# Stick-breaking attention: weights taken as differences of one scan, summed by parts

## The chip, the cores and the metric

The kernel runs on one core of a Trainium2 chip. The metric is the device time of one launch in microseconds (us), as the median of several runs; the kernel before takes 988.35 us (three runs, 987.6 to 989.67).

## The reference

One layer of a streaming encoder. The prompt has 1024 tokens, and 64 new tokens of a running stream have a past of 512; both are computed in the same launch. Per token: RMS norm, one input projection from 1024 to 6144 columns (queries, keys, values and a SiLU gate z for each of two attention branches of 8 heads of 64, and two merge gates), the two attentions, their projections, a gated sum and an output projection with the residual. The branch that is changed is stick breaking:

```python
z = einsum("bqhd,bkhd->bhqk", q, k) * 0.125          # causal: key position < query position
log_keep = where(causal, log_sigmoid(-z), 0.0)
suffix = cumsum(log_keep, axis=3, reverse=True) - log_keep
w = where(causal, exp(log_sigmoid(z) + suffix), 0.0)
out = einsum("bhqk,bkhd->bqhd", w, v)
```

In words: with keep = sigmoid(-z) the weight of key s is sigmoid(z[s]) times the product of keep over all keys between s and the query. Call P[s] the product of keep from s up to the query. Then the weight of s is also P[s+1] - P[s].

## The kernel before

All large products are split into a high and a low part of the fast float format, three matmuls for one. The work has five phases: a first projection by rows (line 464), a second projection computed with seven block products in place of eight (line 634), the two attentions with the remaining eight projection units woven in (lines 663 to 1231), the branch projections, and the output projection.

**The second projection** (lines 544 to 657) takes 12 column pairs with seven steps each, 84 steps of 24 matmuls. `prep` cuts a block of weights into halves five steps ahead of its use: ScalarE makes the high half, GpSimd the low one. `emit` evaluates finished sums into one of four `hl` buffers, and `soon` and `step` put the stores of these into SyncE's queue at the next step. SyncE issues nearly all transfers of the kernel in program order; an issue that has to wait holds back all behind it.

**The attention loop** (line 1189) goes over 136 items: first stick breaking, then band attention, in each four pairs of heads, in each the 64 new tokens (t = 8, both heads at once) and then eight query blocks of 128 for each of the two heads. An item of stick breaking has up to 1024 keys. At loop step i:

- `qk(i)` makes the scores (line 1033); ScalarE takes two sigmoids of them, of -z into `kp` (line 1036) and of z into `be` (line 1037);
- `mid(i-1)` runs VectorE's scan over the keys from right to left, multiplying by `kp` and adding a table `imp` that has a one at the query's own place and zeros elsewhere (line 1056): it yields P. Then `be` is multiplied by P shifted by one key (line 1057);
- `tr(i-3)` transposes `be` in blocks of 128 on TensorE (line 1088), and ScalarE copies these to SBUF (line 1097);
- `av` multiplies by the values (line 1127), and VectorE multiplies the sum by the gate z (line 1132); `store_later` puts the store of it into a list that `flush` empties at the next step.

Between these, `fill(n)` issues n matmuls of the remaining projection units (line 782): 336 over the stick-breaking items, in shares by item length, after 144 in six blocks of 24 that stand ahead of the loop while the first queries, keys and values are loaded (line 1174). Each unit has 72 matmuls in three column groups; a group's end puts one to three stores (line 695) in the list. At a unit's second group, `W.split` cuts the next unit's weights, the low half on GpSimd (line 122). The last unit reads the stick-breaking outputs back from DRAM afterwards, so `fill` is held before it until `late["sb"]` is set at a fixed loop step (line 1218).

All engines take their instructions in the order of the program. TensorE's order is the one in which these functions are called.

The functions in question:

Of the kernel before, what the change touches and what calls it, by code (L numbers as in the profile page):

```python
# [8 lines left out]
F32 = mybir.dt.float32  # L9
# [23 lines left out]
def hybrid_step_kernel(ctx: ExitStack, tc: tile.TileContext, x_prompt, x_sample, c_sbk, c_sbv, c_cbk, c_cbv,  # L33
# [41 lines left out]
    d_sbv = dram.tile([T, 512], F32, name="d_sbv")  # L75
    d_cbv = dram.tile([T, 512], F32, name="d_cbv")
# [467 lines left out]
    with ExitStack() as ph:  # L544
# [60 lines left out]

        load_raw(2)
# [8 lines left out]
        for i in range(len(pairs)):  # L615
            bank, s1, u2, u3 = {}, {}, {}, {}
            for s in range(7):
# [7 lines left out]
                step()  # L625
                w = blk.pop(n)
# [50 lines left out]
    V.tensor_copy(imp[:, 896:1024], ident)  # L677
    ims = ax.tile([128, 576], F32, name="ims", bufs=1)
    G.memset(ims[:, 0:512], 0.0)
    for h in (slice(0, 64), slice(64, 128)):  # L680
        V.tensor_copy(ims[h, 512:576], ident[h, h])
# [12 lines left out]
    def store_later(dst, src):  # L694
        deferred.append((0, lambda: SP.dma_start(dst, src)))
# [34 lines left out]
    def load_v(b, p):  # L730
        src, cache = (d_sbv, c_sbv) if b == "sb" else (d_cbv, c_cbv)
        c = slice(p * 128, (p + 1) * 128)
        vp = am.tile([128, 8, 128], F32, name="vp", bufs=2)
        vs = am.tile([128, 5, 128], F32, name="vs", bufs=1)
        SP.dma_start(vp, src[0:NP, c].rearrange("(t q) c -> q t c", q=128))
        SP.dma_start(vs[:, 0:4], cache[:, c].rearrange("(t q) c -> q t c", q=128))
        SP.dma_start(vs[0:64, 4], src[NP:T, c])
        VP[b, p] = (vp, vs)
# [270 lines left out]
    def qk(i):  # L1009
# [10 lines left out]
        if b == "sb":  # L1020
            kp = ax.tile([128, NP + 2], F32, name="kp", bufs=3)
            G.memset(kp[:r, n:n + 1], 0.0)
        else:
            kp = am.tile([128, 4], F32, name="sm", bufs=6)
            bt = BI[2 * p + hd] if t < 8 else BI["s", p]
            off = 0 if t == 8 else 640 - n
        for j, (x, y) in enumerate(hs):
# [7 lines left out]
            if b == "sb":  # L1035
                A.activation(kp[:r, x:y], z[:r, :m], AF.Sigmoid, scale=-0.125)  # L1036
                A.activation(be[:r, x:y], z[:r, :m], AF.Sigmoid, scale=0.125)  # L1037
# [3 lines left out]
        st[i] = (be, kp)  # L1041
# [7 lines left out]
    def mid(i):  # L1049
# [4 lines left out]
        if b == "sb":  # L1054
            im = ims[:] if t == 8 else imp[:, NP - n:NP]
            V.tensor_tensor_scan(kp[:r, n - 1::-1], kp[:r, n - 1::-1], im[:, ::-1], 0.0, op0=OP.mult, op1=OP.add)  # L1056
            V.tensor_tensor(out=be[:r, :n], in0=be[:r, :n], in1=kp[:r, 1:n + 1], op=OP.mult)  # L1057
# [44 lines left out]
    def load_z(b, p, j):  # L1102
        zt = am.tile([128, 256], F32, name="zt", bufs=3)
        nq = 256 if j < 4 else 64
        SP.dma_start(zt[:, :nq], d_z[b][p][:, 256 * j:256 * j + nq])
        zts[b, p, j] = zt

    def av(b, p, j):
# [23 lines left out]
        V.tensor_tensor(out=os[:, :nq], in0=o[:, :nq], in1=os[:, :nq], op=OP.mult)  # L1132
        store_later(d_o[b][p][:, 256 * j:256 * j + nq], os[:, :nq])
# [47 lines left out]
    n_sb = 72 * 5 - 24  # L1181
# [7 lines left out]
    for i in range(len(seq) + LAG + 1):  # L1189
# [28 lines left out]
        if i < len(seq) and seq[i][:3] == ("cb", 0, 1) and hd == 1:  # L1218
            late["sb"] = True
# [301 lines left out]
```

## Time and profile before

| | |
|---|---|
| median of three runs | 988.35 us (987.6 to 989.67) |
| the profiled execution | 986.78 us, its span 985.0 us |
| TensorE clock granted over the span | 1.00 |
| busy matmul, share of the span | 98% |
| busy VectorE, ScalarE, GpSimd | 64%, 52%, 35% |

The profile is of one execution. A line such as `L1057 DVE ... x68 | 57.3, 843 | 9.4` tells the line of the kernel, the engine, the operation, tile written and tiles read, the count, then busy us in all, mean ns of one, and how long the engine stood idle just before them and what ended that. PE is TensorE's matmul, PEld its weight load, DVE VectorE, ACT ScalarE, POOL GpSimd and SPq SyncE's queue. A timeline row gives the start in us, the duration, engine, line, tiles and count. A matmul's end is modelled, so where a matmul waited is read best from starts.

### The profile page before, as it was taken

How to read it: one execution, taken by the hardware profiler on the slowest of the kernel's cores; microseconds unless marked ns; L12 is line 12 of the kernel's file. 1: busy time of each engine (PE TensorE's matmuls, PEld its weight loads, DVE VectorE, ACT ScalarE, POOL GpSimd, SP SyncE). 2: the span in 40 equal slices, each digit the busy share in tenths (PEclk: the TensorE clock that was granted, in tenths of full speed). 3: DMA queues.
4: the chain of work that ended last, by engine and by line, in shares of the span. 5: the costliest groups of instructions: out<-in, count | busy, mean ns of one | idle time of the engine just before them, and what ended most of it. 6: DMA issues, size and time to landing. Idle time of an engine off the chain costs nothing.

```text
span 985.0 us, 20439 instructions
## 1 busy us (share of the span) xinstructions
PE 962.0 (98%) x7568; PEld 917.6 (93%) x7568; DVE 630.1 (64%) x1188; ACT 510.4 (52%) x1142; POOL 346.2 (35%) x356
## 2 busy tenths in 40 slices
PE   5999999999999999999999999999999999999998
PEld 5999999999999999999998888898888888999998
DVE  5456665696454655532239898997767765599735
ACT  5534443344443433433248787786876875466220
POOL 3376664115444554444211101101201101486641
PEclk9999999999999999999999999999999999999999
DMA  6727567533656333343298656666898772852642
GB/s 229 223 89 243 193 223 253 166 103 120 180 174 203 115 110 101 99 124 99 79 244 221 172 160 161 164 187 169 232 262 226 213 221 68 264 177 83 210 131 86
DMA packets 174243, 166.97 MB, mean 170 GB/s; under 512 B 34688, under 2 KB 160000, under 8 KB 174016
## 3 DMA queue, kind: packets, MB, share of 16 engines
q1 hardware_dynamic: 165424, 157.34, 53.7%
q10 hardware_dynamic: 8720, 8.33, 2.6%
q8 instruction: 60, 0.98, 0.4%
q14 instruction: 39, 0.32, 0.1%
HBM read 106.89 MB, written 58.72 MB: 168 GB/s over the span
## 4 chain that ended last, share of the span: by engine, by line
PE 90%; DMA 3%; ACT 3%; DVE 1%; SPq 1%; issue 1%; POOL 1%; DVEq 0%; ACTq 0%
PE b L634 25%; PE acc L464 19%; PE b L1435 8%; PE o L1127 7%; PE acc L782 7%; PE z L1033 6%; PE pt L1088 6%; PE b L924 5%; PE acc L882 3%; DMA wrawx<-in_w_in_dram 1%; PE pk L349 1%; ACT wT L1097 1%; PE pt L277 1%; SPq L51 1%; PE acc L1471 1%
## 5 line engine op out<-in xcount | busy, mean ns | idle before, releaser
L122 POOL TENSOR_TENSOR wlo<-wraw,whi 128x1024 fp32r<-128x1024 f32 x22 | 57.6, 2618 | 103.0 <-ACT whi L115 102.9
L1088 PE MATMUL pt<-ident,be 128*128 128x128 f32 (+1 forms) x568 | 87.2, 278 | 5.7 <-ACT wT L1097 1.9
L1056 DVE TENSOR_TENSOR_SCAN kp<-kp,imp 128x128 f32<-128x128 f32 (+7 forms) x64 | 88.3, 1379 | 0.6 <-ACT kp L1036 0.6
L1033 PE MATMUL z<-ks,sq 128*128 128x320 f32 (+5 forms) x384 | 83.2, 325 | 0.0
L1088 PEld LDWEIGHTS pt<-ident,be 128*128 128x128 f32 (+1 forms) x568 | 65.9, 140 | 16.8 <-issue 5.7
L1097 ACT ACTIVATE wT<-pt 128x512 f32<-128x512 f32 (+3 forms) x125 | 58.6, 501 | 39.0 <-PE pt L1088 38.9
L464 PE MATMUL acc<-whi,xa 128*128 128x256 f32 x256 | 74.2, 292 | 0.0
L464 PE MATMUL acc<-wlox,xm 128*128 128x256 f32 x256 | 70.8, 278 | 0.0
L464 PE MATMUL acc<-whi,xm 128*128 128x256 f32 x256 | 70.8, 278 | 0.0
L464 PE MATMUL acc<-wlo,xa 128*128 128x256 f32 x256 | 70.7, 278 | 0.0
L464 PE MATMUL acc<-whix,xb 128*128 128x256 f32 x256 | 70.7, 278 | 0.0
L464 PE MATMUL acc<-whix,xm 128*128 128x256 f32 x256 | 70.6, 278 | 0.0
L1033 PEld LDWEIGHTS z<-ks,sq 128*128 128x128 f32 x384 | 65.8, 188 | 1.1 <-issue 0.2
L1127 PE MATMUL o<-wT,vp 128*64 128x256 f32 (+1 forms) x608 | 66.7, 357 | 0.1
L782 PE MATMUL acc<-xm,whi 128*128 128x384 f32 (+1 forms) x192 | 65.2, 340 | 0.0
L1127 PEld LDWEIGHTS o<-wT,vp 128*64 128x64 f32 x608 | 42.3, 136 | 23.9 <-issue 5.7
L1057 DVE TENSOR_TENSOR be<-be,kp 128x128 f32<-128x128 f32 (+8 forms) x68 | 57.3, 843 | 9.4 <-ACT sg L757 0.5
L1036 ACT ACTIVATE kp<-z 128x384 f32<-128x384 f32 (+6 forms) x104 | 52.4, 504 | 9.5 <-PE z L1033 4.5
L642 DVE TENSOR_TENSOR u<-b,s 128x256 f32<-128x256 f32 (+1 forms) x48 | 20.8, 439 | 56.3 <-PE b L634 55.2
L1037 ACT ACTIVATE be<-z 128x384 f32<-128x384 f32 (+6 forms) x104 | 52.9, 508 | 0.0
L1060 ACT ACTIVATE be<-be,sm 128x640 f32<-128x640 f32 (+5 forms) x68 | 47.2, 694 | 9.5 <-DVE sm L1059 9.2
L1047 ACT ACTIVATE be<-be,sm 128x640 f32<-128x640 f32 (+5 forms) x68 | 47.2, 694 | 3.7 <-DVE sm L1039 3.4
(300 smaller groups left out, 3147.4 us busy)
## 6 DMA issues: line engine op xcount, KB each, us to landing
wraw<-in_w_in_dram SPq DMA_DIRECT2D x32, 512.0 KB, 4.6
wrawx<-in_w_in_dram SPq DMA_DIRECT2D x16, 512.0 KB, 4.5
sq<-d_qsbT SPq DMA_DIRECT2D x32, 192.0 KB, 3.6
sq<-d_qcbT SPq DMA_DIRECT2D x32, 192.0 KB, 4.4
xt<-in_x_prompt_dram SPq DMA_DIRECT2D x8, 512.0 KB, 5.8
d_kcbT<-hl SPq DMA_DIRECT2D x8, 512.0 KB, 4.4
d_qcbT<-hl SPq DMA_DIRECT2D x8, 512.0 KB, 5.7
d_ksbT<-hl SPq DMA_DIRECT2D x16, 256.0 KB, 2.5
```

The costliest lines, as they stand in the source:

```text
L122: (eng or G).tensor_tensor(out=l, in0=raw, in1=h[:].bitcast(F32), op=OP.subtract)
L464: TE.matmul(ps, x, w, start=m == 0, stop=m == len(steps) - 1)
L634: TE.matmul(ps[:, :m], w[:, hl_, k], right[s](x)[:, k, a:b], start=s < 3 and k == 0 and e == 0, stop=k == 3 and e == 2, skip_group_check=s ...
L782: TE.matmul(ps[:, :b - a], w[:, k], xk(x, k)[:, a:b], start=k == 0 and n == 0, stop=k == KT - 1 and n == 2)
L1033: TE.matmul(z[:, :m], s[:, e, q0:q0 + 128], ks[:, h, o + x:o + y], start=e == parts[0][0], stop=e == parts[-1][0])
L1037: A.activation(be[:r, x:y], z[:r, :m], AF.Sigmoid, scale=0.125)
L1056: V.tensor_tensor_scan(kp[:r, n - 1::-1], kp[:r, n - 1::-1], im[:, ::-1], 0.0, op0=OP.mult, op1=OP.add)
L1057: V.tensor_tensor(out=be[:r, :n], in0=be[:r, :n], in1=kp[:r, 1:n + 1], op=OP.mult)
L1088: TE.transpose(pt[:kr, x, :r], be[:r, kb * 128:kb * 128 + kr], ident[:r, :r])
L1097: A.activation(w[:, sl:sl + m, q0:q0 + r], pt[:, :m, :r], AF.Copy)
L1127: TE.matmul(o[hd * 64:hd * 64 + 64, c0:c1], vv[:kr, kb, hd * 64:hd * 64 + 64], wT[b, p, j, hd, s // 4][:kr, s % 4, c0:c1] if j < 4 else wT ...
L1435: TE.matmul(ps[:, t], left[s](xs_, k)[:, ts_], wt_[:, k], start=s < 3 and t == k == e == 0, stop=k == 3 and e == 2, skip_group_check=s > 2 ...
```

## The change

The sum over keys of (P[s+1] - P[s]) v[s] is summed by parts: it equals the sum of P[s] (v[s-1] - v[s]) and one remaining value at the end. So the scan's result itself is what is transposed and multiplied, and the values are replaced by differences of neighbouring rows.

- One sigmoid, of -z, written into `be`; `kp`, its memset and the second sigmoid go. The scan works in place on `be`, and the product after it goes.
- The tables `imp` and `ims` now have ones from the query's own place to the end of its block, and the scan takes the maximum in place of the sum: P is one there, so what remains at the end is the last value row of the query's block of 128, the same for all its queries. Nine such rows (eight blocks, and the new tokens) are loaded (`load_vl`), transposed on TensorE into a column for each block (`make_vl`) and added in `av`, where the product with the gate becomes an add and a multiply in one instruction for each 128 queries. Both stand in the six blocks of fill ahead of the loop: `load_vl` after the fifth, `make_vl` after the sixth.
- A table of differences `d_dv` is made in DRAM during the second projection, in 26 jobs of 128 rows by 256 columns (12 blocks and a tail, for each half of the columns): two loads on SyncE, a subtraction on GpSimd, a store on SyncE. From the third column pair on, odd steps load and even steps subtract.
- During stick breaking, the low halves of the woven units' weights are made by VectorE in place of GpSimd.
- The outputs' stores are put off by one more step, `zt` has four buffers in place of three, and `late["sb"]` is set one loop step later (step 73 in place of 72). The count of fill matmuls, 336, is the same.

```diff
+        def dv_load(r0, rows_, cur, prev, c):
+            a, b = (up.tile([128, 256], F32, name=x, bufs=2) for x in ("dva", "dvb"))
+            if len(prev) == 1 and prev[0] is None:
+                G.memset(a[0:1], 0.0)
+                SP.dma_start(a[1:rows_], cur[0:rows_ - 1, c])
+            else:
+                o = 0
+                for q in prev:
+                    SP.dma_start(a[o:o + q.shape[0]], q[:, c])
+                    o += q.shape[0]
+            SP.dma_start(b[:rows_], cur[:, c])
+            dvs.append((r0, rows_, c, a, b))
+
+        def dv_sub():
+            r0, r, c, a, b = dvs.pop(0)
+            G.tensor_tensor(out=a[:r], in0=a[:r], in1=b[:r], op=OP.subtract)
+            soon(0, lambda: SP.dma_start(d_dv[r0:r0 + r, c], a[:r]))
...
+        def dv_step(load):
+            if load and dv_jobs:
+                dv_load(*dv_jobs.pop(0))
+            elif not load and (len(dvs) > 1 or dvs and not dv_jobs):
+                dv_sub()
...
                 step()
+                if i > 1:
+                    dv_step(n % 2)
...
-    V.tensor_copy(imp[:, 896:1024], ident)
+    V.tensor_tensor_scan(imp[:, 896:1024], ident, ident, 0.0, op0=OP.max, op1=OP.max)
...
+    def load_vl():
+        SP.dma_start(vrow[0:8], d_sbv[0:NP].rearrange("(t q) c -> t q c", q=128)[:, 127])
+        SP.dma_start(vrow[8:9], d_sbv[T - 1:T])
+
+    def make_vl():
+        pt = psT.tile([128, 4, 128], F32, name="pt")
+        for p in range(NPAIR):
+            TE.transpose(pt[:, p, 0:9], vrow[0:9, p * 128:(p + 1) * 128], ident[0:9, 0:9])
+        V.tensor_copy(vl[:, :, 0:9], pt[:, :, 0:9])
...
-    def store_later(dst, src):
-        deferred.append((0, lambda: SP.dma_start(dst, src)))
+    def store_later(dst, src, n=0):
+        deferred.append((n, lambda: SP.dma_start(dst, src)))
...
-        src, cache = (d_sbv, c_sbv) if b == "sb" else (d_cbv, c_cbv)
+        src, cache, n0 = (d_dv, d_dv[NP:NP + PAST], NP + PAST) if b == "sb" else (d_cbv, c_cbv, NP)
...
-                            W.split(("u", j + 1) if j + 1 < len(units) else ("p", 0))
+                            W.split(("u", j + 1) if j + 1 < len(units) else ("p", 0), None if "sb" in late else V)
...
-        if b == "sb":
-            kp = ax.tile([128, NP + 2], F32, name="kp", bufs=3)
-            G.memset(kp[:r, n:n + 1], 0.0)
-        else:
+        if b == "cb":
...
-                A.activation(kp[:r, x:y], z[:r, :m], AF.Sigmoid, scale=-0.125)
-                A.activation(be[:r, x:y], z[:r, :m], AF.Sigmoid, scale=0.125)
+                A.activation(be[:r, x:y], z[:r, :m], AF.Sigmoid, scale=-0.125)
...
-            V.tensor_tensor_scan(kp[:r, n - 1::-1], kp[:r, n - 1::-1], im[:, ::-1], 0.0, op0=OP.mult, op1=OP.add)
-            V.tensor_tensor(out=be[:r, :n], in0=be[:r, :n], in1=kp[:r, 1:n + 1], op=OP.mult)
+            V.tensor_tensor_scan(be[:r, n - 1::-1], be[:r, n - 1::-1], im[:, ::-1], 0.0, op0=OP.mult, op1=OP.max)
...
-        V.tensor_tensor(out=os[:, :nq], in0=o[:, :nq], in1=os[:, :nq], op=OP.mult)
-        store_later(d_o[b][p][:, 256 * j:256 * j + nq], os[:, :nq])
+        if b == "sb":
+            for x in range(0, nq, 128):
+                y = min(x + 128, nq)
+                c = 2 * j + x // 128
+                V.scalar_tensor_tensor(os[:, x:y], o[:, x:y], vl[:, p, c:c + 1], os[:, x:y], op0=OP.add, op1=OP.mult)
+        else:
+            V.tensor_tensor(out=os[:, :nq], in0=o[:, :nq], in1=os[:, :nq], op=OP.mult)
+        store_later(d_o[b][p][:, 256 * j:256 * j + nq], os[:, :nq], 1)
...
     load_k("sb", 0, 1)
     for f in (lambda: load_q("sb", 0, 3), lambda: load_k("sb", 0, 0), lambda: load_q("sb", 0, 0),
-              lambda: (load_v("sb", 0), load_z("sb", 0, 4)), lambda: None, lambda: None):
+              lambda: (load_v("sb", 0), load_z("sb", 0, 4)), load_vl, lambda: None):
         fill(24)
         flush()
         f()
+    make_vl()
...
-        if i < len(seq) and seq[i][:3] == ("cb", 0, 1) and hd == 1:
+        if i == len(seq) // 2 + LAG + 2:
             late["sb"] = True
```

More of the change, by code (lines that the diff above doesn't have):

```diff
@@ L75, in hybrid_step_kernel @@
     d_sbv = dram.tile([T, 512], F32, name="d_sbv")
+    d_dv = dram.tile([T + PAST, 512], F32, name="d_dv")
     d_cbv = dram.tile([T, 512], F32, name="d_cbv")
@@ L680, in hybrid_step_kernel @@
     for h in (slice(0, 64), slice(64, 128)):
-        V.tensor_copy(ims[h, 512:576], ident[h, h])
+        V.tensor_tensor_scan(ims[h, 512:576], ident[h, h], ident[h, h], 0.0, op0=OP.max, op1=OP.max)
+    vl = ax.tile([128, NPAIR, 16], F32, name="vl", bufs=1)
+    vrow = ax.tile([16, 512], F32, name="vrow", bufs=1)
+    def load_vl():
[6 more added lines that the diff above has]
+        V.tensor_copy(vl[:, :, 0:9], pt[:, :, 0:9])
     deferred = []
@@ L1102, in load_z @@
     def load_z(b, p, j):
-        zt = am.tile([128, 256], F32, name="zt", bufs=3)
+        zt = am.tile([128, 256], F32, name="zt", bufs=4)
         nq = 256 if j < 4 else 64
@@ L1179, in hybrid_step_kernel @@
         f()
+    make_vl()
     FP = 180
-    n_sb = 72 * 5 - 24
+    n_sb = 336
     n_cb = 72 * (len(units) - 2) - n_sb + FP
```

12 lines of the change are left out of this document (10 added, 2 removed).

## The prediction

> **What bounds the kernel now.** I read the page first, then busy time by stage, then the stage that the change touches, instruction by instruction, and last the DMA queue and the landings ahead of it.
>
> ```profile
> PE 962.0 (98%) x7568; PEld 917.6 (93%) x7568; DVE 630.1 (64%) x1188; ACT 510.4 (52%) x1142; POOL 346.2 (35%) x356
> ...
> PE 90%; DMA 3%; ACT 3%; DVE 1%; SPq 1%; issue 1%; POOL 1%; DVEq 0%; ACTq 0%
> ```
>
> TensorE is busy for 98% of the span and carries 90% of the chain that ended last. So time is lost or won only where a matmul waits; work taken from VectorE or ScalarE is worth what it frees there. Busy time by stage (us, then PE, PEld, DVE, ACT, POOL, clock, DMA share, GB/s):
>
> ```profile
> 227.40:483.10 255.70, 255.70 (x2059) 254.83 (x2058) 119.20 (x232) 99.54 (x228) 121.45 (x84) 1.00 0.43 129
> ...
> 506.70:683.00 176.30, 173.24 (x1283) 151.83 (x1283) 156.05 (x167) 139.22 (x341) 22.22 (x74) 1.00 0.69 183
> 683.00:835.00 152.00, 148.63 (x1149) 128.80 (x1145) 104.71 (x383) 109.76 (x246) 17.00 (x22) 1.00 0.71 199
> ```
>
> The first stretch is the Strassen-like second projection phase, the next the stick-breaking part, the third the band part. In the stick-breaking part VectorE has 156.05 of 176.30 us and ScalarE 139.22, which looks like the bound, yet TensorE is idle for only 176.30 - 173.24 = 3.06 us: fill matmuls are dosed so that all three run level. In the projection phase TensorE has no gap at all.
>
> **The change, part by part.** What goes, from the groups:
>
> ```profile
> L1056 DVE TENSOR_TENSOR_SCAN kp<-kp,imp 128x128 f32<-128x128 f32 (+7 forms) x64 | 88.3, 1379 | 0.6 <-ACT kp L1036 0.6
> ...
> L122 POOL TENSOR_TENSOR wlo<-wraw,whi 128x1024 fp32r<-128x1024 f32 x22 | 57.6, 2618 | 103.0 <-ACT whi L115 102.9
> L1057 DVE TENSOR_TENSOR be<-be,kp 128x128 f32<-128x128 f32 (+8 forms) x68 | 57.3, 843 | 9.4 <-ACT sg L757 0.5
> L1037 ACT ACTIVATE be<-z 128x384 f32<-128x384 f32 (+6 forms) x104 | 52.9, 508 | 0.0
> ```
>
> *Second sigmoid and product.* 104 x 508 ns = 52.9 us leave ScalarE, 68 x 843 ns = 57.3 us leave VectorE, and 68 one-column memsets leave GpSimd, which waits there anyway. All of it lies beside TensorE; worth what stalls remain. The first stall of the stage, in TensorE's order of time:
>
> ```profile
> 506.71 1.22 PE L1033 MATMUL z<-kss,sqs 128*128 128x288 f32 x8
> 507.77 0.34 PE L782 MATMUL acc<-xa,whi 128*128 128x384 f32 x1
> 507.95 0.34 PE L782 MATMUL acc<-xm,whi 128*128 128x384 f32 x1
> ...
> 509.68 0.34 PE L782 MATMUL acc<-xm,whi 128*128 128x384 f32 x1
> 510.85 0.77 PE L1088 MATMUL pt<-ident,be 128*128 128x128 f32 x5 [0.84 <-DVE be L1057]
> ```
>
> The transposes wait for the product. A fill matmul of 384 columns starts 0.17 us after the one before it elsewhere in this stage (507.77 and 507.95 us), so of the 1.17 us between 509.68 and 510.85 some 1.0 is lost where the view says 0.84, because matmul ends are modelled. Scaled so, the stage's 3.06 us idle are 3.06 x 1.0/0.84 = 3.7 us, mostly at the start of each head pair, where VectorE is behind after the long rows. With a third of its work gone it is not behind any more. Term: **-3.7 us**; ends 0 (the next late engine takes the place at once) and -4.6 (half of the 1.8 us of waits that some matmuls hide as longer spacing added).
>
> What is added to VectorE has these rows beside it, a full product of 1024 columns and the output's product:
>
> ```profile
> L1057 DVE TENSOR_TENSOR be<-be,kp 128x1024 f32<-128x1024 f32 x8 | 11.7, 1461 | 1.1
> ...
> L1132 DVE TENSOR_TENSOR zt<-o,zt 128x256 f32<-128x256 f32 (+1 forms) x21 | 7.8, 372 | 9.5 <-PE o L1127 9.4
> ```
>
> *The scan* reads and writes `be` with max in place of add: the same 1379 ns, 0. If max were dearer, VectorE's 156.05 - 57.3 us leave 77 us of cover, so up to 1.8 times the 88.3 us costs nothing. *The output*: 20 products become 36, each of 128 columns; 16 more at under 372 ns is 6 us of VectorE in the same cover, 0. *Low halves of weights* move from GpSimd (2618 ns each) to VectorE for about six units: 6 x 1.5 us, in the same cover, 0. The two mask tables, now built by three scans, lie ahead of any reader, 0. *Loading values* from the new table moves the same bytes, 0. *Deferred stores* and the fourth `zt` buffer take a wait out of SyncE's queue; the gate for the last fill unit opens one step later, which holds back one step's fill, one to two matmuls of 0.17 us: **+0.2**, ends 0 and +0.7. The fill count stays 336.
>
> *The table of differences* is made in the projection phase: 26 jobs, each two loads, one GpSimd subtraction of 128x256 and one store, 80 DMAs in SyncE's queue and, for four jobs, a memset.
>
> ```profile
> L434 POOL TENSOR_TENSOR whix<-ws,whix 128x512 fp32r<-128x512 f32 x24 | 31.7, 1321 | 34.7 <-ACT whix L433 34.7
> ...
> SPq L389 <- DVE ws L401: 46.8, 11, 4.9
> ...
> ACT hl L572 <- DMA d_zsb<-hl: 3.9, 2, 2.1
> ...
> 340.52 0.45 DVE L649 TENSOR_TENSOR u<-b,u 128x288 f32<-128x288 f32 x1
> ...
> 344.39 0.30 PE L634 MATMUL b<-t0l,whix 128*128 128x288 f32 x1
> ```
>
> GpSimd: 26 x 0.7 us (half of 1321 ns) = 18 us beside 121.45 of 255.70 us busy; weights are cut five steps ahead, so it is hidden. SyncE is the doubtful one. A load into a buffer waits until the store two jobs before has landed, some 2 us, every second step of 3 us, with the stores of `hl` queued behind it; ScalarE already waits for such stores (2.1 us at worst, here), and DVE's reading of the bank then ends at 340.97, 3.4 us before TensorE writes that bank again (344.39). One or two us more waiting fits in that. Term: **+0.5 us**, ends 0 and +6 (below).
>
> *The last values.* Two row loads (`load_vl`) are queued after the fifth block of 24 fill matmuls, and after the sixth TensorE transposes them (`make_vl`) ahead of the first score matmul. That is the one place where the change gives TensorE a new wait, and everything behind it on the engine waits too. SyncE and ScalarE there:
>
> ```profile
> 502.59 0.43 SPq L735 DMA_DIRECT2D vp<-d_sbv  x1
> ...
> 505.40 1.24 SPq L109 DMA_DIRECT2D wraw<-in_w_in_dram  x1
> 506.73 3.96 SPq L695 DMA_DIRECT2D d_gcb<-sg  x5
> 510.74 5.17 SPq L51 DMA_DIRECT2D sq<-d_qsbT  x8
> ...
> 503.45 0.49 ACT L757 ACTIVATE sg<-acc 128x384 f32<-128x384 f32 x1 [2.75 <-issue]
> ```
>
> The sixth block ends at 506.71, where the first `z` starts. The five stores at 506.73 are three pieces of the fifth block and two of the sixth; `load_vl` goes between them. The first store of the five holds the queue long, the other four take under 0.5 us each (3.96 us in all), so the third ends near 506.73 + 3.96 - 2 x 0.46 = 509.8, and the two row loads are issued at 509.8 and 510.3. How long until they land, from the queue's issues between 506.5 and 511 us, and for comparison the shortest median landing of the page:
>
> ```profile
> d_gcb<-sg SPq DMA_DIRECT2D x1, 112.0 KB, 3.4
> ...
> d_gcb<-sg SPq DMA_DIRECT2D x2, 16.0 KB, 3.4
> ...
> d_gsb<-hl SPq DMA_DIRECT2D x32, 128.0 KB, 1.7
> ```
>
> Even 16 KB takes 3.4 us there: vp, vs and a weight block of 512 KB are ahead. So the rows land by 509.8 + 3.4 = 513.2 to 513.7 us and TensorE, ready at 506.71, stands for **+6.8 us** (513.5 - 506.7). Nothing covers it: fill comes after the transposes in its order. Lower end: stores queued as soon as the fifth block's `sg` is there (503.45 + 0.49 = 503.94), five issues at 0.45 us, 1.7 us to land: 507.9, a stall of 1.2. Upper end 7.5, if the two rows take the whole queue's turn after the stores. The four transposes themselves: 4 x 0.11 us (128-column transposes run five in 0.77 above) = **+0.45**.
>
> *The clock after such a pause.* The end and the start of the run show what idling does:
>
> ```profile
> 981.00:982.00 1.00, 0.24 (x3) 0.05 (x1) 0.69 (x1) 0.00 (x0) 0.00 (x0) 1.00 0.01 2
> ...
> 984.00:985.00 1.00, 0.00 (x0) 0.00 (x0) 0.00 (x0) 0.00 (x0) 0.00 (x0) 0.98 0.00 0
> 985.00:986.00 1.00, 0.00 (x0) 0.00 (x0) 0.00 (x0) 0.00 (x0) 0.00 (x0) 0.50 0.00 0
> ...
> 11.70 1.22 PE L464 MATMUL acc<-whi,xs 128*128 128x256 f32 x4 [2.16 <-ACT whi L115]
> ...
> 15.28 0.77 PE L464 MATMUL acc<-wlo,xs 128*128 128x256 f32 x4
> ...
> 19.38 0.63 PE L464 MATMUL acc<-whix,xm 128*128 128x256 f32 x4
> ```
>
> The last matmul ends at 981.24; the granted clock falls to 0.50 just before 985, after 3.7 us. At the start four matmuls of 256 columns take 1.22 us at 11.70 and 0.63 at 19.38, and the faster spacing begins with the four at 15.28: about half speed for the first 3.6 us of steady work. A pause of 6.8 us is longer than 3.7, so I expect half speed for some 3.6 us after it, losing half of that: **+1.8 us**, ends 0 (pause under 3.7 us) and +3.6. The Trainium skill, TensorE: Matmul & The Clock Gate, section "What's actually happening", says the same of an idle window and of a busy window, each of about 3.4 us; by its figure the term would be 1.7. The trace's 3.7 and 3.6 us agree with it.
>
> **Sum.** -3.7 + 0.2 + 0.5 + 6.8 + 0.45 + 1.8 = +6.05 us. The profiled execution took 986.78 us (span 985.0 and 1.8 around it), 1.6 us under the median of 988.35. The terms come from it, so its like would be 992.8; on the median it is 988.35 + 6.05 = **994.4 us**.
>
> **The rivals.**
> *A, the forecast*: the pause of TensorE outweighs the stalls removed. 994.4; own range 990.5 to 997.5 (clock term 0 and scarcely 3 us of gain, or all terms at their upper ends but the projection phase).
> *B, not slower*: the queue is clear when `load_vl` comes, and the rows land at 507.9. It decides when they land before about 510.4 us, 3.7 us after 506.7: then no clock is lost and the stall equals the gain. At the lower end: -3.7 + 1.2 + 0.45 + 0.2 + 0.5 = -1.35, 987.0; with -4.6 and nothing in the projection phase 985.4. For it: the two loads are tiny. Against it: the 3.4 us of the 16 KB stores at this very place.
> *C, the projection phase gives way*: `hl` stores held behind the new waits come so late that a bank is not read in time. The point is the 3.4 us shown above. Rows that speak for it: 46.8 us in which SyncE already stands before a weight load. Four loads have 127 rows (the first row of each column half is zero), and would do it most easily if they went through one engine:
>
> ```profile
> 160.00:170.00 10.00, 10.00 (x87) 10.00 (x87) 2.58 (x8) 3.03 (x7) 2.39 (x1) 1.00 1.02 362
> ```
>
> 362 GB/s on 16 full engines is 22.6 GB/s each, so 127 rows of 1 KB on one are 5.8 us, with every later store's share on that engine behind them; 5.8 - 3.4 = 2.4 us of stall for the two of the four that come while `hl` is written, about 5 us with some ordinary waits: 994.4 + 5.5 = 999.9. The Trainium skill, DMA: Bandwidth & Descriptors, section "Why a DMA increments its semaphore by 16 and not by 1", states that a transfer runs on as many engines as divide its row count, and on a single one for 127. No run so far shows such a row count, so the rule stands as a reason for C alone.
> *D, the change does not do what it says*: the stalls of the stick-breaking part come from elsewhere (chain latency) and stay; 994.4 + 3.7 = 998.1. Against it: the product is the named releaser of the first.
>
> **How the numbers follow.** A 0.63, B 0.17, C 0.14, D 0.06. A change of 0.2%, 2.0 us, is about what a measurement of this kernel can tell from none: 986.4 to 990.3. Faster: 0.6 of B, 0.10. Same: the rest of B and A's low edge, 0.14. Slower: 0.76. The range of 8 in 10 runs from 987.0 (B's nearer half) to 1000.0 (C's price).
>
> **What would show it.** In the profile after: a gap of 6 to 7 us on TensorE before the four new transposes near 506.7 us, ended by the DMA of `vrow`; a granted clock of 0.5 in the us after it; no wait of 0.5 us or more before the transposes at the later head pairs; VectorE near 110 us in the stage. The prediction is wrong if the transposes of `vrow` start before 510 us, or if the projection phase, 255.7 us now, is longer by over 2 us.

## The result, and the profile after

The changed kernel takes **998.7 us** (median of 4 runs, 995.85 to 1000.55) against 988.25 us for the kernel before: a ratio of **1.0101, 95% interval 1.0075 to 1.0128**. Its profiled execution took 995.85 us, span 994.1.

The page of the changed kernel, its busy line, the line of the chain that ended last, and the groups of the scan and of the one sigmoid that is left:

```profile
PE 965.1 (97%) x7572; PEld 919.2 (92%) x7572; DVE 595.6 (60%) x1144; ACT 474.8 (48%) x1038; POOL 340.7 (34%) x311
...
PE 85%; DMA 5%; issue 3%; DVE 2%; POOL 2%; ACT 2%; SPq 1%; POOLq 0%; ACTq 0%; DVEq 0%
...
L1101 DVE TENSOR_TENSOR_SCAN be<-be,imp 128x128 f32<-128x128 f32 (+7 forms) x64 | 85.7, 1351 | 13.2 <-ACT be L1082 12.7
...
L1082 ACT ACTIVATE be<-z 128x384 f32<-128x384 f32 (+6 forms) x104 | 47.0, 485 | 24.6 <-PE z L1079 23.7
```

VectorE and ScalarE each lose some 35 us of work over the run (630.1 to 595.6 and 510.4 to 474.8), and the time still goes up: both were beside TensorE. A scan with max costs what a scan with add did, 1351 against 1379 ns. TensorE's share of the chain falls from 90 to 85%, and what it lost went to DMAs and to the issue of instructions. Busy time by stage in the changed kernel (us of the stretch, then PE, PEld, DVE, ACT, POOL, clock, DMA share, GB/s), the second projection, the stick-breaking part and the band part:

```profile
226.20:487.10 260.90, 257.75 (x2060) 255.46 (x2059) 125.93 (x232) 98.81 (x229) 141.78 (x114) 1.00 0.54 164
517.10:692.00 174.90, 173.99 (x1282) 153.09 (x1283) 107.82 (x120) 103.72 (x236) 0.58 (x4) 0.99 0.69 180
692.00:844.50 152.50, 149.56 (x1150) 129.51 (x1147) 106.60 (x384) 109.71 (x246) 17.35 (x22) 1.00 0.70 195
```

In the stick-breaking part TensorE's idle time falls from 3.06 to 0.91 us. The second projection, where TensorE had no gap at all, now has 3.15 us without a matmul. And the stages do not join: the projection ends at 487.10, the 144 fill matmuls end at 510.8, and the first score matmul starts at 517.10. TensorE's order of time there:

```profile
510.51 0.30 PE L831 MATMUL acc<-xm,wlo 128*128 128x320 f32 x1
516.61 0.56 PE L729 MATMUL pt<-ident,vrow 9*128 9x9 f32 x4 [5.79 <-DMA vrow<-d_sbv]
517.10 2.29 PE L1079 MATMUL z<-kss,sqs 128*128 128x288 f32 x8
519.18 0.52 PE L831 MATMUL acc<-xa,whi 128*128 128x384 f32 x1
519.50 0.52 PE L831 MATMUL acc<-xm,whi 128*128 128x384 f32 x1
```

TensorE stands for 5.79 us until the last value rows land. The first eight score matmuls then take 2.29 us where they took 1.22 before, and fills follow each other at 0.32 us where they did at about 0.18. SyncE's queue and the granted clock (last number but two of a window) at that place:

```profile
510.39 2.66 SPq L744 DMA_DIRECT2D d_gcb<-sg  x3
513.10 0.33 SPq L723 DMA_DIRECT2D vrow<-d_sbv  x1
513.80 0.23 SPq L724 DMA_DIRECT2D vrow<-d_sbv  x1
```

```profile
514.00:516.00 2.00, 0.00 (x0) 0.00 (x0) 0.00 (x0) 0.00 (x0) 0.00 (x0) 0.50 0.55 159
516.00:518.00 2.00, 1.40 (x8) 1.40 (x9) 0.20 (x1) 0.00 (x0) 0.00 (x0) 0.50 0.44 124
518.00:520.00 2.00, 2.00 (x9) 2.00 (x9) 0.08 (x1) 0.82 (x2) 0.00 (x0) 0.50 1.02 250
520.00:522.00 2.00, 2.00 (x14) 1.98 (x13) 1.85 (x3) 0.56 (x2) 0.00 (x0) 0.82 1.06 243
```

The two row loads leave SyncE behind three stores, 2.3 and 3.0 us after TensorE is ready, and TensorE goes on 2.8 us after the second. The clock stands at 0.50 until about 520.7.

The gaps of the second projection have one large member. SyncE, ScalarE and TensorE around it, in the changed kernel:

```profile
334.61 0.26 SPq L613 DMA_DIRECT2D dva<-in_cache_sb_v_dram  x1
334.92 0.50 SPq L619 DMA_DIRECT2D dvb<-in_cache_sb_v_dram  x1
335.51 2.36 SPq L570 DMA_DIRECT2D d_zsb<-hl  x3
```

```profile
343.03 0.42 ACT L573 ACTIVATE hl<-s 128x256 f32<-128x256 f32 x1 [8.50 <-DMA d_zsb<-hl]
```

```profile
344.33 0.41 PE L671 MATMUL b<-t1h,wlo 128*128 128x288 f32 x1 [2.13 <-DVE s L683]
```

```profile
342.00:343.00 1.00, 0.20 (x2) 0.00 (x0) 0.00 (x0) 0.00 (x0) 0.00 (x0) 1.00 0.08 27
```

L613 is a load of 127 rows. The stores queued behind it hold ScalarE for 8.50 us (a buffer `hl` comes free only when they have landed; 2.1 us was the longest wait for `d_zsb` before), VectorE reads its bank late for that, and TensorE waits 2.13 us for the bank. Just before the stores land the core's 16 DMA engines are busy for a share of 0.08, little over one sixteenth, and move 27 GB/s.

Where the time went, stretch by stretch, from the first matmul of each stage in the profiled executions (us; "to the scores" is from the end of the second projection to the first score matmul, pairs are head pairs of stick breaking):

| | second projection | to the scores | pair 1 | pairs 2 to 4 | first two band pairs | span |
|---|---|---|---|---|---|---|
| before | 255.8 | 23.6 | 37.0 | 129.8 | 79.5 | 985.0 |
| after | 260.9 | 30.0 | 37.7 | 127.8 | 79.5 | 994.1 |

So +5.1, +6.4, +0.7, -2.0 and 0.0. Of the 5.1 us the view shows 3.15 as time without a matmul; the rest is matmuls spaced wider, and what held those isn't shown. The first projection and the output projection at the end, whose code is the same in both, are 2.0 us shorter after. Two of the experiments below ran the kernel before with an addition elsewhere, and they have the shorter times too, so that is scatter of the one profiled execution of before. The rest, +0.8 in the later band pairs, is no larger than that scatter.

### The profile page after: what moved, and what is told of

It is laid out like the page before. It is cut to its first block, busy times and chain, and to the rows that moved or that the text cites. A ratio compares the mean times of both kernels' runs of the same rounds, so it can differ in the third digit from the quotient of the medians.

```text
span 994.1 us, 20328 instructions
## 1 busy us (share of the span) xinstructions
PE 965.1 (97%) x7572; PEld 919.2 (92%) x7572; DVE 595.6 (60%) x1144; ACT 474.8 (48%) x1038; POOL 340.7 (34%) x311
## 4 chain that ended last, share of the span: by engine, by line
PE 85%; DMA 5%; issue 3%; DVE 2%; POOL 2%; ACT 2%; SPq 1%; POOLq 0%; ACTq 0%; DVEq 0%
PE acc L465 19%; PE b L671 17%; PE acc L831 9%; PE b L1486 8%; PE o L1171 7%; PE z L1079 7%; PE pt L1132 6%; PE b L973 5%; PE acc L931 4%; DMA d_dv<-dva 2%; PE pk L350 1%; DMA wrawx<-in_w_in_dram 1%; DMA gt<-d_gsb 1%; PE pt L278 1%; DMA d_ksbT<-hl 1%
## 5 line engine op out<-in xcount | busy, mean ns | idle before, releaser
L1101 DVE TENSOR_TENSOR_SCAN be<-be,imp 128x128 f32<-128x128 f32 (+7 forms) x64 | 85.7, 1351 | 13.2 <-ACT be L1082 12.7
L123 POOL TENSOR_TENSOR wlo<-wraw,whi 128x1024 fp32r<-128x1024 f32 x15 | 36.0, 2402 | 68.3 <-ACT whi L116 68.2
L1082 ACT ACTIVATE be<-z 128x384 f32<-128x384 f32 (+6 forms) x104 | 47.0, 485 | 24.6 <-PE z L1079 23.7
L465 PEld LDWEIGHTS acc<-whi,xa 128*128 128x128 f32 x256 | 47.9, 188 | 0.1
```

What stands on the lines that cost most here:

```text
L465: TE.matmul(ps, x, w, start=m == 0, stop=m == len(steps) - 1)
L1101: V.tensor_tensor_scan(be[:r, n - 1::-1], be[:r, n - 1::-1], im[:, ::-1], 0.0, op0=OP.mult, op1=OP.max)
```

## Experiments

Each ratio is against runs of the kernel before on the same chip, with its 95% interval.

**1. The last value rows early.**

```diff
+    load_vl()
     load_k("sb", 0, 1)
...
-              lambda: (load_v("sb", 0), load_z("sb", 0, 4)), load_vl, lambda: None):
+              lambda: (load_v("sb", 0), load_z("sb", 0, 4)), lambda: None, lambda: None):
```

> Changed kernel, with the two loads of the last value rows (load_vl) issued before the first key strips of stick breaking instead of behind the fifth group of 24 fills. Theory P (TensorE stands still for the rows, because their loads stand in SP's queue behind stores that are still waiting): the 5.8 us wait ahead of the four transposes and the time at half clock behind it both go; the stretch from the last work of the projection to the first score matmul falls from 30.0 to about 24 us, and stick breaking loses some 1.7 us more: about 8 us in all, 998.7 to about 990.7 us. Rival Q (the rows only hide the next late thing, the scores' own strips, or the two extra loads push those back): the pause stays at 3 us or more in front of the first score matmul, and the time stays above 995 us. If the clock at half speed is not tied to the pause, only the 6 us go: 992.5 us.

Measured: 991.98 us, ratio 1.0051 (1.0036 to 1.0065), against 1.0101 for the changed kernel: 0.50%, 4.9 us, is back. TensorE's first steps and its next wait, in this kernel:

```profile
513.76 0.41 PE L729 MATMUL pt<-ident,vrow 9*128 9x9 f32 x4
514.10 1.31 PE L1079 MATMUL z<-kss,sqs 128*128 128x288 f32 x8
...
523.64 0.70 PE L1079 MATMUL z<-ks,sq 128*128 128x512 f32 x2 [0.88 <-DMA sq<-d_qsbT]
```

Theory P holds for the pause: no wait before the transposes, eight scores in 1.31 us, 24.0 us to the scores instead of 30.0. The 1.7 us expected from the clock did not come: pair 1 takes 37.9 us, no less than the 37.7 after the pause. The second query strip, issued while the pause lasted in the changed kernel, is now the late thing (0.88 us by the view). The projection happened to lose 3.1 us more than in the changed kernel's profile (264.0 against 260.9), so its stalls are not of one size.

**2. Loads of 127 rows in two.**

```diff
-                SP.dma_start(a[1:rows_], cur[0:rows_ - 1, c])
+                SP.dma_start(a[1:113], cur[0:112, c])
+                SP.dma_start(a[113:rows_], cur[112:rows_ - 1, c])
```

> Changed kernel, with each load of 127 rows for the table of differences made as two, of 112 and of 15 rows. Theory S (the 127 rows lie on one DMA engine, and the stores behind them wait for it): TensorE's 2.3 us stall at 341.9 us goes, and the second projection falls from 260.9 to about 258 us; the time from 998.7 to about 996 us. Rival B (the loads wait for buffers, with SP's queue behind them, whatever their rows): the projection stays within 0.5 us of 260.9 and the time within 1 us of 998.7, and the 2.3 us stall is found again.

Measured: 993.7 us, ratio 1.0063 (1.0048 to 1.0078): 3.8 us back from four loads split. ScalarE behind the same stores, and the stretch 330 to 400 us, which had 67.43 us of matmuls in 70 in the changed kernel:

```profile
337.15 0.42 ACT L573 ACTIVATE hl<-s 128x256 f32<-128x256 f32 x1 [3.62 <-DMA d_zsb<-hl]
```

```profile
330.00:400.00 70.00, 69.84 (x559) 69.60 (x558) 39.57 (x78) 25.64 (x58) 44.80 (x38) 1.00 0.56 170
```

The wait for the stores shrinks from 8.50 to 3.62 us, and nearly all of the idle time goes; the projection takes 257.7 us. So far theory S holds, with a gain in the time somewhat above the 2.7 us that I had expected.

**3 and 4. One part alone, on the kernel before.** Experiment 3 adds only `load_vl` and `make_vl`; experiment 4 adds only the jobs of the table.

```diff
     prologue of the kernel before (experiment 3)
-              lambda: (load_v("sb", 0), load_z("sb", 0, 4)), lambda: None, lambda: None):
+              lambda: (load_v("sb", 0), load_z("sb", 0, 4)), load_vl, lambda: None):
...
+    make_vl()
     second projection of the kernel before (experiment 4)
                 step()
+                if i > 1:
+                    dv_step(n % 2)
```

> Kernel before, with only the loads of the last value rows, the four transposes of them and the copy added, at the places that they have in the changed kernel; nothing uses the result. Theory P: TensorE waits about 6 us for the rows and then runs some 7 us at half clock, as in the changed kernel: 988.3 + 6.4 + 1.7 = 996.4 us. Rival Q (the pause of the changed kernel comes from stores that the change itself made late, so that the rows are there in time on the kernel before): under 2 us of wait, 988 to 990.5 us.

> Kernel before, with only the 26 jobs of the table of differences added to the second projection; stick breaking still reads the values themselves, so the table is made and not used. Theory T (the table's loads and stores, in SP's queue and on the DMA engines, are what slows the projection): the second projection grows from 255.8 to about 260.9 us, and the time from 988.3 to about 993.3 us, in stalls of TensorE between 290 and 380 us. Rival U (the projection is slower for another reason in the change, such as the work split or buffers placed otherwise): the projection stays within 1 us of 255.8 and the time within 1 us of 988.3.

Measured: 996.65 us, ratio 1.0083 (1.0065 to 1.01), for the rows; 994.45 us, ratio 1.0075 (1.006 to 1.0089), for the table. TensorE with the rows added:

```profile
511.54 0.56 PE L693 MATMUL pt<-ident,vrow 9*128 9x9 f32 x4 [5.58 <-DMA vrow<-d_sbv]
512.03 2.29 PE L1046 MATMUL z<-kss,sqs 128*128 128x288 f32 x8
```

and the same stretch of the projection with the table added:

```profile
330.00:400.00 70.00, 66.00 (x524) 65.36 (x525) 37.24 (x69) 23.22 (x52) 40.99 (x36) 1.00 0.50 153
```

Both costs appear without the rest of the change: the pause with 29.8 us to the scores and 1.0 us more in pair 1 (theory P), the projection at 265.2 us (theory T). Rivals Q and U fall. Together they cost 1.58%, 15.6 us, more than the 1.01% of the whole change, so the rest of the change brings something.

**5. Four buffers for the table's tiles.**

```diff
-            a, b = (up.tile([128, 256], F32, name=x, bufs=2) for x in ("dva", "dvb"))
+            a, b = (up.tile([128, 256], F32, name=x, bufs=4) for x in ("dva", "dvb"))
```

> Changed kernel, with four buffers instead of two for each of the two tiles of the table's jobs, so that a load waits for the store of four jobs before. Loads of 127 rows stay as they are. Theory S (one DMA engine drains the 127 rows, and what is queued behind them is late): no change, the second projection 260.9 to 264 us as seen twice, the time within 1.5 us of 998.7. Rival B (loads that wait for their buffers hold up SP's queue): the projection falls to 258 us or less and the time to about 995.5 us.

Measured: 992.58 us, ratio 1.0035 (1.0019 to 1.0052), with the projection at 256.4 us and the pause still there (5.21 us). I had expected theory S to hold alone, and it did not: the 127 rows go as before, and the stall is gone. The longest waits of SyncE's queue in the projection in the changed kernel:

```profile
SPq L617 <- DMA d_dv<-dva: 39.9, 16, 5.9
SPq L570 <- ACT hl L573: 25.5, 13, 8.3
```

and the same place as in experiment 2, with four buffers:

```profile
328.76 0.29 SPq L613 DMA_DIRECT2D dva<-in_cache_sb_v_dram  x1
329.10 0.86 SPq L619 DMA_DIRECT2D dvb<-in_cache_sb_v_dram  x1
330.06 3.19 SPq L570 DMA_DIRECT2D d_zsb<-hl  x3
```

```profile
338.30 0.42 ACT L573 ACTIVATE hl<-s 128x256 f32<-128x256 f32 x1 [4.17 <-DMA d_zsb<-hl]
```

SyncE no longer stands 39.9 us for stores of two jobs before, so the 127 rows and the stores behind them are issued 5.5 to 5.9 us sooner (328.76 against 334.61, 330.06 against 335.51). The stores still take about 8 us to free the buffer (330.06 to 338.30; 335.51 to 343.03 in the changed kernel), but they end in time. Each of the two things uses up room, and most of the stall takes both. The loads split alone do not always end it: two later kernels with two buffers still had 0.4 us (experiment 6) and 1.4 us (experiment 7) without a matmul.

**6, 7 and 8. The edits together, and the change without its table.** Experiment 6 has the edits of 1 and 2. Experiment 7 adds this:

```diff
+              lambda: (load_v("sb", 0), load_z("sb", 0, 4)), lambda: load_q("sb", 0, 1), lambda: None):
...
         if t == 8:
-            load_q(b, p, 1)
+            if (b, p) != ("sb", 0):
+                load_q(b, p, 1)
```

Experiment 8 has the rows and the strip early, and no `dv_step`; its `load_v` reads the values themselves, so the kernel leaves the differences out.

> Changed kernel with both edits of the first two experiments: the last value rows loaded early, and the loads of 127 rows made as 112 and 15. If the two costs lie in different stretches and add up: 998.7 - 6.7 - 5.0 = 987.0 us, with the second projection at about 257.7 us and 24 us to the first score matmul. If one of the two gains was the other's (the pause absorbs what is late from the projection): 990 us or more. The wait of some 0.9 us for a query strip at 522 us in the first experiment should be found again, some 6 us earlier.

> As the kernel with both edits, and the second query strip of the first head pair is loaded in the place among the fills that the value rows have left free, instead of behind the first score tile. Theory N (the strip is the next late thing, behind five stores in SP's queue): the stall of 0.9 us in front of the scores that read it goes, with 0.5 to 1.5 us of the time: about 986 us, 1 to 2 us below the kernel before. Rival (its four transfers only push back the value and gate loads behind them, so that the products with the values wait in its place): within 0.5 us of the kernel with both edits.

> Changed kernel with the value rows and the second strip early, and without the jobs of the table: stick breaking reads the values themselves, so the differences of neighbouring values are left out of the result. It shows what the arithmetic of the change alone brings and what the table costs when its loads are split: by my sum 988.0 - 3.7 + 0.5 for transposes + 0.2 = 985 us, with the second projection at 255.8 us; the table split costs the difference to the kernel with the strip early, 0.5 us by my sum, 1 us at most by the traces. If stick breaking had gained nothing: 988.5 us.

Measured: 987.64 us, ratio **0.9983 (0.9971 to 0.9994)** for 6; 987.13 us, 0.9985 (0.9973 to 0.9997) for 7; 986.05 us, 0.9969 (0.9958 to 0.9981) for 8. The two main costs lie in different stretches: 1.18% comes back where the two edits alone gave 0.50 and 0.38%, and the pause did not hide what the projection lost. That it is more than the sum stays open; the stalls of the projection differ from execution to execution (260.9 and 264.0 us above, 256.9 in experiment 6). Without the two costs the change is 0.17% faster than before. Moving the strip did not pay by the time: its wait shrank by the view from 0.88 us (experiment 1) to 0.58, since stores and the values were still ahead of it in the queue. The projection without the table, and with it in experiment 7:

```profile
226.16:483.26 257.10, 257.10 (x2059) 256.24 (x2058) 119.83 (x232) 99.86 (x229) 120.05 (x84) 1.00 0.43 128
```

```profile
225.90:484.86 258.96, 257.55 (x2059) 256.02 (x2058) 121.94 (x232) 99.33 (x229) 140.94 (x114) 1.00 0.55 165
```

With the loads split the table still cost 1.4 us of stalls in that execution. What the change brings without its table, the strip moved as well, is 0.31% (0.19 to 0.42), about 3 us, where the terms of my sum for it (-3.7, +0.2 and +0.45) make 3.05. That the totals agree doesn't confirm the terms: in the two profiled executions pairs 2 to 4 are some 2 us shorter, but pair 1 is 0.4 and the way to the scores 0.5 us longer, so about 1 us of the 3 is located and the rest is not.

**9 and 12. All edits, in two orders.** Both have the edits of 1, 2 and 5 and the strip of 7. Experiment 9 loads the strip ahead of the first values and gates, experiment 12 behind them.

```diff
     experiment 9
+              lambda: load_q("sb", 0, 1), lambda: (load_v("sb", 0), load_z("sb", 0, 4)), lambda: None):
     experiment 12
+              lambda: (load_v("sb", 0), load_z("sb", 0, 4)), lambda: load_q("sb", 0, 1), lambda: None):
```

> Changed kernel with all edits: the last value rows early, loads of 127 rows made as 112 and 15, four buffers for the table's tiles, and the second query strip of the first pair loaded ahead of the first values and gates. Theory J (the projection had about as much room as one of two things takes, the loads' waits for a store or the 127 rows on one engine, and is slowed only by both): no more than the kernel with the loads split and the strip early gives, up to 2 us less where its projection still had stalls of 1.9 us: 985 to 987 us. The wait of 0.6 us for the strip goes; if the values come late for it, a wait of similar size stands in front of the products with the values.

> The kernel with all edits, with the first values and gates loaded ahead of the second query strip again. If the 5.4 us wait of that kernel is the values' loads, pushed back behind the strip in SP's queue: it goes, and the strip's wait of 0.6 us comes back; the stretch of the first head pair falls from 42.8 to about 37 us, the projection stays at 256 to 257 us, and the time is 985 to 986 us, 2 to 3 us below the kernel before. If the four buffers make the values late in another way: 991 us again.

Measured: 991.18 us, ratio 1.0034 (1.0023 to 1.0045), for 9; **986.16 us, ratio 0.9978 (0.9965 to 0.9991)** for 12. In 9 the strip was in time and TensorE stood for the values:

```profile
516.22 1.53 PE L1172 MATMUL o<-wT,vs 128*64 128x64 f32 x20 [5.26 <-DMA vs<-d_dv]
```

Pair 1 took 42.8 us. I had foreseen a wait of the strip's size, 0.6 us, and it was nine times that. In 12 the values wait 0.56 us and the strip 0.50, pair 1 takes 37.5 us, and the projection, in the view by stretches,

```profile
226.17:481.90 255.73, 255.73 (x2059) 254.87 (x2058) 120.84 (x232) 99.57 (x229) 141.24 (x114) 1.00 0.56 167
```

has no gap again, with the whole table made and the DMA share at 0.56 against 0.43 before; so the bytes of the table are not what slowed it. This version beats both kernels: 2.2 us under the one before by its ratio, and 12 us under the changed one by the two ratios. Experiments 6 and 7 beat both too, and the intervals don't tell the three apart.

**10. Every load as 127 rows and 1 row.** On the kernel of experiment 9:

```diff
-                for q in prev:
+                for q in [y for x in prev for y in ((x[0:127], x[127:128]) if x.shape[0] == 128 else (x,))]:
```

> The kernel with all edits, but each of the 22 loads of 128 rows for the table that was one transfer is made as 127 rows and 1 row. Theory S (127 rows go through one DMA engine, and the stores behind them land some 4 us later): the projection gets stalls of TensorE at many of these loads, 1 to 2 us each where the room of that pair is used up, and grows by 5 to 20 us; time 990 to 1005 us. If the split of the 127 rows had helped only by its timing, a load of 127 rows costs no more than one of 128: within 1.5 us of the kernel with all edits.

Measured: 1035.23 us, ratio 1.0473 (1.0457 to 1.0489): 44 us over the kernel of experiment 9, twice the most that I had expected (and from 20 loads: I had counted 22). One place of it, by TensorE and by windows:

```profile
328.99 0.61 PE L672 MATMUL b<-t1h,wlo 128*128 128x288 f32 x1 [8.85 <-DVE s L684]
```

```profile
322.00:324.00 2.00, 0.00 (x0) 0.00 (x0) 0.00 (x0) 0.00 (x0) 0.00 (x0) 1.00 0.97 329
324.00:326.00 2.00, 0.00 (x0) 0.00 (x0) 0.00 (x0) 0.00 (x0) 0.00 (x0) 0.80 0.27 70
326.00:328.00 2.00, 0.00 (x0) 0.00 (x0) 0.00 (x0) 0.31 (x1) 0.72 (x1) 0.50 0.07 23
```

TensorE stands for 8.85 us, and before it goes on the DMA engines run at a share of 0.07 and 23 GB/s: what one engine of sixteen (0.0625) makes while the other fifteen are idle. My prediction had 22.6 GB/s for one engine, worked out from 362 GB/s on all. The Trainium skill, DMA: Bandwidth & Descriptors, section "Why a DMA increments its semaphore by 16 and not by 1", gives a single engine for 127 rows. The trace agrees, with 23 GB/s here and 27 GB/s at 342 us of the changed kernel. This kernel has a 1-row transfer more at each of these loads, so not all 44 us are the 127 rows' alone; the windows show only that one engine is what is waited for at this place.

**11. The gate as before.** On the kernel of experiment 9:

```diff
-        if i == len(seq) // 2 + LAG + 2:
+        if i < len(seq) and seq[i][:3] == ("cb", 0, 1) and hd == 1:
```

> The kernel with all edits, with the point from which the projection's matmuls are spread over the late work put back to where the kernel before has it (the second head of the first tile of the second branch). By my sum the later point costs 0.2 us: the time goes down by 0.2 us, which the runs can't tell. Rival (the later point is what makes the first pair of the second branch 1.6 us longer): the first pair falls back from 42.3 to 40.7 us, the second one rises from 37.3 to 38.7 us, as in the kernel before, and the sum of both moves by less than 0.5 us.

Measured: 992.96 us, ratio 1.0047 (1.0031 to 1.0063), whose interval overlaps that of experiment 9. The first two band pairs with the gate as before:

```profile
678.11:718.84 40.73, 40.10 (x311) 35.34 (x311) 25.27 (x90) 31.04 (x70) 6.37 (x8) 1.00 0.62 178
718.84:758.42 39.58, 37.21 (x285) 32.37 (x284) 27.84 (x102) 29.13 (x70) 5.71 (x8) 1.00 0.84 238
```

and in the kernel of experiment 9:

```profile
676.88:719.24 42.36, 41.04 (x312) 35.65 (x311) 26.77 (x90) 32.13 (x73) 6.25 (x8) 1.00 0.72 201
719.24:756.53 37.29, 36.97 (x284) 32.37 (x283) 27.66 (x102) 27.93 (x66) 5.71 (x8) 1.00 0.85 235
```

The later gate moves fill from the second pair to the first; the sum of both is 79.65 us with it and 80.31 without. That is no gain shown: the kernel before has 79.5 us with the early gate, and the changed kernel 79.5 with the late one. The time of the runs doesn't settle it either.

## Why the prediction was right, and where it was not

I predicted 994.4 us, +6.05, and it was 998.7, +10.45 on the medians of one comparison. It lies in the range, and the direction and the pause of forecast A are shown. But it is over A's own range, which ended at 997.5: rival C, whose price was 999.9, came true on top of A, and the time is in the range only because that was drawn up to C's price. (A's end of 997.5 keeps the stalls at -3.7; with every term but the projection's at its upper end the sum is 1001.1.) The text had said that the prediction is wrong if the projection grows by over 2 us, and it grew by 5.1. Term by term, from the profiled executions:

- **The pause for the last rows, +6.8.** Right. The stretch to the scores grew by 6.4 us, transposes included; TensorE idles 5.79 us by the view, and moving the two loads took 6.0 us away (experiment 1). The loads came later than I had them (513.1 and 513.8 against 509.8 and 510.3), but TensorE was ready later too, at 510.8 against 506.7, because the slower projection pushed everything back, so the difference held.
- **The clock, +1.8.** Near as loss, too large as cost. From the first score matmul to the first transposes TensorE took 4.88 us (517.10 to 521.98) where the same work takes 3.27 without the pause (514.10 to 517.37 in experiment 1): 1.6 us lost. It was 2.0 and 2.7 us in experiments 2 and 5, which keep the pause, because the clock stayed at 0.50 for 4.9 and 6.4 us after TensorE went on, against 4.1 in the changed kernel and 3.6 in my sum. Pair 1 follows it: 38.1 and 38.7 us, against 37.7. But part of what TensorE lost, the loads behind it gained: without the pause pair 1 is no shorter than 37.8 to 37.9 us in the same order of loads (experiments 6 and 1), since TensorE then waits for the query strip. As cost it is between 0 and 1 us.
- **The table, +0.5.** This is the step that failed: "One or two us more waiting fits in that." ScalarE's longest wait for the stores was 8.50 us, and the projection lost 5.1 us (and 3.1 and 4.3 us more than that in experiments 1 and 4). I had both causes and left them out of the sum. The waits for the store two jobs before were named and priced at some 2 us, and one is about that (39.9 us in 16 waits, 2.5 each); what I left out is that the same stores are also late behind the 127 rows. Those I gave to rival C with 5.8 us on one engine, and held a chance of 0.14 for it, since no row of the trace of before showed such a load. The two together made the term; either of them alone left the projection at 256 to 259 us (experiments 2, 5, 6 and 7), from about the 0.5 that I took to some 3 us. The waits in the queue are no cost by their sum: with the loads split, 31.0 us of them in 16 waits stayed, and TensorE had 0.16 us without a matmul in the projection (experiment 2).
- **Stalls of stick breaking, -3.7.** Half right. In pairs 2 to 4, 2.0 us went, in every kernel with the new scan. The waits there in the kernel before were these:

```profile
548.54 0.63 PE L1088 MATMUL pt<-ident,be 128*128 128x128 f32 x4 [0.35 <-ACT wT L1097]
591.07 0.66 PE L1088 MATMUL pt<-ident,be 128*128 128x128 f32 x4 [0.65 <-ACT wT L1097]
635.33 0.85 PE L1088 MATMUL pt<-ident,be 128*128 128x128 f32 x6 [0.51 <-DVE be L1057]
```

Two of the three ended with ScalarE's copy and one with VectorE's product, where I had put them to VectorE alone. The change takes work from both engines, and no run separates which of it did it. The 1.0 us at the start of pair 1, which waited for the product, went too, but there the next late thing stands close: the values and the second strip, 0.56 and 0.50 us in experiment 12. So "ends 0 (the next late engine takes the place at once)" was true of pair 1, and the next late one was a load and no engine. VectorE has 107.8 us in the stage, as foreseen ("near 110"), and the longest wait of the changed kernel in front of the transposes of pairs 2 to 4 is this one, 0.27 us:

```profile
600.68 1.09 PE L1132 MATMUL pt<-ident,be 128*128 128x128 f32 x8 [0.27 <-ACT wT L1141]
```

- **The late gate, +0.2.** Not measurable, neither in the time nor by the two band pairs (experiment 11).
- **Transposes, +0.45.** Right: 0.56 us at half clock, 0.41 at full (experiment 1).
- **Edits at nothing.** The max scan (1351 against 1379 ns), the output in more pieces and the weights on VectorE stayed hidden, as far as the whole shows it: TensorE has 0.91 us without a matmul in the stage, and with the two stalls out of the way the kernel is faster than before. None of them was run by itself.

Rival B (rows there at 507.9) is excluded by the landing. Rival D (the stalls stay) had a price of 998.1, nearest of all to the time, and is excluded by pairs 2 to 4 alone. Three slips in the working change none of this: 3.06 x 1.0/0.84 is 3.6, B's lower price is 985.6 unless the gate's 0.2 goes as well, and C's 5.5 is about 5 by its own stalls.

## What to carry to other kernels

When a change moves work to the DMA queues, take the one store that an engine waits for and add up all that delays it, its late issue behind loads that wait for a buffer and its late landing behind a load on one engine, before saying that a buffer's slack covers it. A load of 127 rows should be cut so that it spreads over the engines. And a load that TensorE needs before its next stage is best issued ahead of the stores that wait for that work; moving loads about in one queue only changes which of them is late, as experiments 1, 9 and 12 show.

## What the runs showed of the hardware

- A transfer of 127 rows of 1 KB delays others than itself: stores queued behind it freed their buffer 7.5 and 8.2 us after the first of them was issued (335.51 to 343.03 in the changed kernel, 330.06 to 338.30 in experiment 5), where such a store landed 2.4 us after issue in the median on the kernel before:

```profile
d_zsb<-hl SPq DMA_DIRECT2D x16, 128.0 KB, 2.4
```

- Such a load can also hold SyncE's queue at the issue behind it. In experiment 10 that is a 1-row transfer (2.27 us, the first line below). In the changed kernel it is a load of 128 rows, so it needs no single row: 3.40 us behind the 127 rows at 278.67 us, where the same issue takes 0.35 with the load split (experiment 2):

```profile
326.23 2.27 SPq L618 DMA_DIRECT2D dva<-d_sbv  x1
```

```profile
278.67 0.40 SPq L613 DMA_DIRECT2D dva<-d_sbv  x1
279.12 3.40 SPq L619 DMA_DIRECT2D dvb<-d_sbv  x1
```

- A pause of TensorE of 5.2 to 5.8 us had a loss of 1.6 to 2.7 us behind it at half clock (the changed kernel, experiments 2 and 5), but the kernel paid 0 to 1 us of that, since DMAs that were nearly late caught up. In these and in experiment 3 the clock stood at 0.50 for 6.8 us in all, and how much of that came after the pause went by when it fell: 3.1 us after the last matmul in the changed kernel (510.8 to 513.9), 4.8 in experiment 5 (506.7 to 511.5). The Trainium skill, TensorE: Matmul & The Clock Gate, section "What's actually happening", has a busy window of about 3.4 us before full clock is back, from which I estimate 1.7 us; the loss in the changed kernel agrees with that, those of experiments 2 and 5 are larger, and the cost to the kernel is less.
